# A two-layer diffusion backbone in full fp32: the q-half swap issued by another engine, one more gating half in the last head, and a lagging third projection at the norm boundaries

## Chip, cores, metric

One Trainium2 chip; the kernel runs on one core of it. The metric is the device time of one execution in microseconds (us), given as the median of several runs. TensorE does the matrix products, ScalarE the activations and most copies out of PSUM, VectorE the elementwise work, GpSimd some elementwise work and DMA issues, SyncE only DMA issues.

## The reference, cut to what matters

Two layers work on 512 latent tokens and 256 context tokens of width 1024. In each layer three branches (spatial gating, attention, short convolution) share one projection of the normalised stream; they are gated, merged and projected back, and a convolutional feed-forward block follows. In the second layer the context only gives keys and values.

```python
h_lat = modulate(rmsnorm(x, norm1_g[l]), sh1, sc1)
z_lat = h_lat @ w_in[l]            # 1024 -> 512 u, 512 v, q, k, v, conv, gates
q_lat = apply_rope(qk_heads(z_lat[..., B_Q:B_K], q_norm_g[l]), cos, sin)
...
def diff_attention(q, k, v, lam):  # 8 heads; q and k are 2 x 64 wide, v 128
    s = jnp.einsum('bqahd,bkahd->bahqk', q, k).astype(jnp.float32) * (B_QK_DIM ** -0.5)
    p = jax.nn.softmax(s, axis=-1)
    a = (p[:, 0] - lam * p[:, 1]).astype(v.dtype)
    return jnp.einsum('bhqk,bkhe->bqhe', a, v)
...
def spatial_gating(u, v, ln_g, w_s, b_s):
    u = jax.nn.gelu(u)
    v = layernorm(jax.nn.gelu(v), ln_g)
    ...
y_b = (rmsnorm(attn, sub_g) * (1.0 - lam_init)).reshape(bn, tn, B_WIDTH)
m = g_a * (y_a @ wa) + g_b * (y_b @ wb) + g_c * (y_c @ wc)
```

## The kernel before

**Layout and precision.** Activations lie feature by token: a tile has 128 features on its partitions and up to 768 tokens (512 latent, 256 context) along its row. Every fp32 product is made of three matmuls in a reduced type on a value's high part and its remainder: high times high (L183), high weight times low activation (L184), low weight times high activation (L186). So every operand is split first: ScalarE copies the high part (`whi`, `hh`, `kT`, `qT`, `vh`, `ah`), VectorE subtracts it from the original (`wlo`, `hl`, `vl`, `al`). A score block has the high and low part of a 64-wide half in one 128-row contraction; the second of its two products needs the same q with the halves of the partitions swapped, which is what the q-half swap makes by DMA (L743): rows 0 to 63 of `qT[:, 0]` to rows 64 to 127 of `qT[:, 1]` and the other way round, 64x2x256 each.

**Weights.** They come in halves of 128x1024 in a fixed order: SyncE issues the load (L62, `wraw`), ScalarE writes `whi` (L83), VectorE `wlo` (L69). There are two raw buffers, so a later load waits for the subtraction of an earlier one. `split_to(n)` writes ScalarE's part of the halves up to n at that place of the program, `take` does it for the half that is needed and the next; with `late` set, VectorE's part is written at the next `low()`.

**Order.** Each engine executes its instructions in the order in which the program writes them; that order is made by hand and by `weave`, which takes generators of pieces of work, each with a total cost, and always continues the one that is least advanced in share of its total. SyncE, too, takes its DMA issues in program order.

**Attention, per head.** While head h computes its scores (`attn`), the projections of head h+1 are woven in (`project`). Then comes the turn to the next head: `qk_tr` transposes the scaled and rotated q and k in three chunks of 256 tokens (two of q in layer 1), woven with one filler, a half of the convolution branch (`c_fill`). A chunk of q is copied out of PSUM by ScalarE (L741) and swapped in two DMAs (L743), a chunk of k is copied by ScalarE twice (L747). `v_tr` transposes v and splits it (L780, L781). Then `attn` takes blocks of 128 queries: scores (L857), VectorE's row minimum (L864), ScalarE's exponential (L869), the difference of the two softmaxes, its transposes (`to_at`, with the copy L897 `ah` and L898 `al`) and the product with v (`av`). The last head has no projection to be woven with: it gets the remaining fillers, which are two halves of the gating branch (`vs`, N_VS = 2).

**After the heads.** `branch_a` (spatial gating: the other `vs` halves with their gelu L1063, u, the layer norm's statistics L1086 and L1087, the token mixing) is woven with `subln`, the norm of the attention's output: the squares of all heads (L953) are split (L170, L171), summed over features on TensorE (L968), scaled by VectorE (L973) and transposed (L977).

**Norm boundaries.** `boundary` stands between two blocks, three times in the program. First come the last three projections of the old block on the first part of the tokens and then on the second, with their residuals `resid` (L1179 and the squares behind it, `sq_acc` L323), those of the second part being put off in `todo`. Then, in eight steps k, the normalised stream of the first part is written tile by tile (`norm_apply`: `hh` on ScalarE L376, `hl` on VectorE L379), and the first three projections of the next block use each tile as it comes: `step(k, part, i)` is the product of tile k for projection i. Projections 0 and 1 follow tile by tile; the third lags. `both` holds at the two boundaries inside a layer, where both token parts go through the norm here; between the layers the second part, the context, is left to the attention's start. The second part's statistics (`norm_stat`) start at one of these steps.

Of the kernel before, what the change touches and what calls it, by code (L numbers as in the profile page):

```python
# [11 lines left out]
F32 = mybir.dt.float32  # L12
# [8 lines left out]
NL, NC, T, D = 512, 256, 768, 1024  # L21
# [9 lines left out]
N_HALF = 2 * (NH * 3 + 12 + 4 + 4 + 24 + 8 + 8 + 8 + 44 + 24)  # L31
N_ADA = 4 * 24
N_LAST = 3
N_VS = 2


def weave(*gens, tick=lambda: None):
# [92 lines left out]
class Net:  # L130
# [376 lines left out]
    def boundary(self, pool, l, which, xt, pkeys, segs, evac, tail, xb=None, tmpb=None):  # L507
        parts = self.parts()
        (ao, am, _), (bo, bm, _) = parts
        sc = self.scales(l, which)  # L510
        self.scales_set(sc, l, which)
        both = xb is None
        tmp = lambda: pool.tile([128, T], F32, tag="nsq", bufs=2, name="nt")
        rb = pool.tile([128, T], F32, tag="rb", bufs=1, name="rb")
        rbb = rb[:, bo:bo + bm] if both else xb[8]
        xa = [x[:, ao:ao + am] for x in xt]
        todo = []
        tkeys, ks, xs, resid = tail
        self.ws.late = True
        ws = [self.ws.take(*key, ahead=0 if i else len(tkeys) - 1) for i, key in enumerate(tkeys)]  # L520
        m0 = 8 - len(tkeys)
        for i, w in enumerate(ws):
            ps = self.mm.tile([128, 512], F32, tag="mm", name="mm")
            self.gemm(w, ks, xs, [parts[0]], [ps])
            resid(m0 + i, parts[0], ps)
        for i, w in enumerate(ws):
            ps = self.mm.tile([128, 512], F32, tag="mm", name="mm")
            self.gemm(w, ks, xs, [parts[1]], [ps])
            todo.append(lambda i=i, ps=ps: resid(m0 + i, parts[1], ps))
            if i == 0:  # L530
                ra = self.norm_stat(ao, am)
                self.ws.split_to(len(self.ws.keys) + 1)
                self.defer = []
                todo.pop(0)()
                self.ws.low()
            if i == 1:
                self.norm_rows(rb[:, ao:ao + am], ra, am)
                self.ws.split_to(len(self.ws.keys) + 2)
        self.norm_h()
        step, finish = self.halves(pkeys, segs, evac)  # L540
        ga = self.norm_apply(tmp, sc, xa, rb[:, ao:ao + am], parts[0])
        next(ga)
        self.ws.low()
        self.ws.split_to(len(self.ws.keys) + 3)
        l1, l2 = 1, 2
        for k in range(8):
            if k == 1:
                self.ws.low()
            if both:
                step(k, parts[0], 0)  # L550
                step(k, parts[0], 1)
                if k:
                    step(k - 1, parts[0], 2)
            else:
                for i, lag in enumerate((0, l1, l2)):
                    if k >= lag:
                        step(k - lag, parts[0], i)
            if todo:
                todo.pop(0)()
            if k < 7:  # L560
                next(ga)
            for f in self.defer:
                f()
            self.defer = []
            if k == 3:
                r = self.norm_stat(bo, bm, True)
            if k == 6 and both:
                self.tick(99)
                self.norm_rows(rbb, r, bm)
        self.tick(99)  # L570
        self.defer = None
        if both:
            step(7, parts[0], 2)
        else:
            finish(parts[0], (8, 8 - l1, 8 - l2))
            self.norm_rows(rbb, r, bm)
        self.ws.low()
        self.ws.late = False
        gb = self.norm_apply(tmp if both else tmpb, sc, [x[:, bo:bo + bm] for x in xt] if both else xb, rbb, parts[1])
        if both:  # L580
            for k in range(8):
                next(gb)
                for i, lag in enumerate((0, 2, 4)):
                    if k >= lag:
                        step(k - lag, parts[1], i)
            finish(parts[1], (8, 6, 4))
            gb = None
        return gb
# [134 lines left out]
    def qk_tr(self, l, h, pool, st):  # L723
        nc = self.nc
        qT = pool.tile([128, 2, 2, T], F32R, tag="qT", bufs=1, name="qT")
        kT = [self.slots.tile([128, T], F32R, tag=f"B{1 + a}", name="kT") for a in range(2)]
        y = self.qk_rope(l, 2, pool, st)
        yield 1500
        for c in range(3):
            qs, ks = st.pop(("rope", c))  # L730
            t0 = c * 256
            for v, src in enumerate((qs, ks)):
                if src is None:
                    continue
                pt = self.mm.tile([128, 512], F32R, tag="mm", name="mmT")
                for a in range(2):
                    for b in range(2):
                        nc.tensor.transpose(pt[:, (2 * a + b) * 128:(2 * a + b + 1) * 128], src[:, 2 * b + a, :], self.identr)
                pf = pt.bitcast(F32)
                if v == 0:  # L740
                    nc.scalar.copy(qT[:, 0, :, t0:t0 + 256], pf.rearrange("p (a t) -> p a t", a=2))  # L741
                    for i, j in ((0, 64), (64, 0)):
                        nc.sync.dma_start(qT[i:i + 64, 1, :, t0:t0 + 256].bitcast(F32),  # L743
                                          qT[j:j + 64, 0, :, t0:t0 + 256].bitcast(F32))
                else:
                    for a in range(2):
                        nc.scalar.copy(kT[a][:, t0:t0 + 256], pf[:, 256 * a:256 * a + 256])  # L747
            if c == 0:
                st["rope", 2] = self.qk_hl(*y, pool)
            yield 1700  # L750
        st["q"], st["k"] = qT, kT
# [44 lines left out]
    def c_fill(self, l, pool, scr):  # L796
        nc = self.nc
# [39 lines left out]
            nc.sync.dma_start(scr[i][:, :n], c[:, :n])  # L837
        self.vg = []
        for i in range(N_VS):
            v = self.slots.tile([128, T], F32, tag=("B0", "B7")[i], name="vg")  # L840
            self.vg.append(v)
            yield half(0, i, lambda o, m, q: nc.scalar.copy(v[:, o:o + m], q[:, :m]), "vs")

# [407 lines left out]
    def run(self):  # L1251
        tc, nc, d = self.tc, self.nc, self.d
# [12 lines left out]
        with tc.tile_pool(name="const", bufs=1) as const, tc.tile_pool(name="w", bufs=1) as wp, \  # L1265
# [45 lines left out]
            for l in range(2):  # L1311
# [12 lines left out]
                with tc.tile_pool(name="attn", bufs=1) as ap, tc.tile_pool(name="pmm", bufs=4, space=PSUM) as self.mm, \  # L1324
# [3 lines left out]
                    tick = self.ws.low  # L1328
# [45 lines left out]
                    for h in range(8):  # L1374
                        a = self.attn(l, h, ap, st[h]), sum(self.attn_costs(l))
                        if h < 7:
                            weave(a, (project(h + 1), 23500), tick=tick)
                            turn(h + 1)
                        else:
                            weave(a, (fill(99), (1 + N_VS) * (6000 if l else 10000)), tick=tick)  # L1380
                self.ws.low()
                self.ws.late = False
                mmp = psum_all()
# [187 lines left out]
```

## Time and profile before

| | before |
|---|---|
| time, median of 3 runs | 2674.5 us (2672.96, 2674.5, 2675.52) |
| the profiled execution's own time | 2675.01 us |
| its span | 2673.2 us |
| granted TensorE clock, mean over the span | 0.993 of full speed |
| TensorE matmul busy | 2617.0 us, 98% |
| TensorE weight load busy (beside the matmuls) | 2267.7 us, 85% |
| VectorE busy | 1631.2 us, 61% |
| ScalarE busy | 1035.2 us, 39% |
| GpSimd busy | 220.9 us, 8% |

The span runs from the first to the last instruction on record; the execution's time has 1.8 us around it. Busy shares are means over the whole span; what a stage waits for is read from the waits and the timelines of that stage. In a timeline's row stand the start in us from the span's start, the length, the engine, the line with the operation, what it writes and reads with shapes, and in brackets the idle time in front of it with what ended it. DMA-issuing instructions aren't counted as busy.

### The profile page before, as it was taken

What the parts mean: (1) busy time and instruction counts of PE and PEld (TensorE: products, weight loads), DVE (VectorE), ACT (ScalarE), POOL (GpSimd) and SP (SyncE); (2) the same over time, 40 slices, a digit from 0 to 9 for tenths busy, and PEclk for the clock granted to TensorE, in tenths of its full rate; (3) what the DMA queues carried; (4) which work ended last, traced back from release to release, by engine and by line L of the source; (5) the groups of instructions that cost most, each with busy time, mean ns of one, the idle gap of its engine ahead of it and who ended that gap; (6) DMA issues with size and microseconds to landing.
All of it is one profiled execution on the core that took longest, in us unless ns stands there. A gap on an engine that the chain in (4) does not pass through costs nothing.

```text
span 2673.2 us, 37362 instructions
## 1 busy us (share of the span) xinstructions
PE 2617.0 (98%) x15128; PEld 2267.7 (85%) x15128; DVE 1631.2 (61%) x2887; ACT 1035.2 (39%) x1840; POOL 220.9 (8%) x202
## 2 busy tenths in 40 slices
PE   7999999999999999999999999999999999999999
PEld 3899999888888888888888878898978888888887
DVE  5677777656546447544544567777767564654544
ACT  3455555542121224312312335555563232343422
POOL 0000000001111111100100100000001121010101
PEclk8999999999999999999999999999999999999999
DMA  5212221224333332222222232212125554233233
GB/s 224 82 44 58 64 66 44 66 66 149 113 116 111 103 127 66 76 87 72 79 81 77 91 100 67 68 55 63 53 75 173 175 163 175 71 99 100 94 103 110
DMA packets 79660, 254.36 MB, mean 95 GB/s; under 512 B 9200, under 2 KB 19712, under 8 KB 79104
## 3 DMA queue, kind: packets, MB, share of 16 engines
q1 hardware_dynamic: 64512, 196.64, 23.1%
q0 software_dynamic: 14544, 55.07, 6.4%
q8 instruction: 119, 1.95, 0.3%
q14 instruction: 53, 0.43, 0.1%
q10 hardware_dynamic: 432, 0.27, 0.0%
HBM read 234.63 MB, written 6.82 MB: 90 GB/s over the span
## 4 chain that ended last, share of the span: by engine, by line
PE 82%; DVE 10%; ACT 4%; DMA 2%; issue 1%; SPq 0%; POOL 0%; ACTq 0%; POOLq 0%; DVEq 0%
PE mm L183 22%; PE mm L186 22%; PE mm L184 22%; PE S L857 3%; PE mm L647 2%; PE mm L649 2%; PE mm L648 2%; DVE wlo L69 2%; PE mmT L893 1%; ACT whi L83 1%; DMA qT<-qT 1%; ACT pa L869 1%; DVE zs L697 1%; DVE al L898 1%; PE mmT L906 1%
## 5 line engine op out<-in xcount | busy, mean ns | idle before, releaser
L183 PE MATMUL mm<-hh,whi 128*128 128x512 f32 (+1 forms) x2392 | 855.3, 358 | 12.1 <-ACT hh L376 10.2
L184 PE MATMUL mm<-hl,whi 128*128 128x512 f32 (+1 forms) x2392 | 820.0, 353 | 4.4 <-DVE hl L379 4.1
L186 PE MATMUL mm<-hh,wlo 128*128 128x512 f32 (+1 forms) x2392 | 752.6, 353 | 1.6 <-DVE wlo L69 1.6
L183 PEld LDWEIGHTS mm<-hh,whi 128*128 128x128 f32 x2392 | 452.6, 189 | 104.5 <-ACT hh L376 14.4
L69 DVE TENSOR_TENSOR wlo<-wraw,whi 128x1024 fp32r<-128x1024 f32 x320 | 399.4, 1249 | 195.8 <-ACT whi L83 194.2
L184 PEld LDWEIGHTS mm<-hl,whi 128*128 128x128 f32 x2392 | 453.3, 190 | 68.4 <-DVE hl L379 9.3
L186 PEld LDWEIGHTS mm<-hh,wlo 128*128 128x128 f32 x2392 | 415.1, 190 | 42.1 <-DVE wlo L69 3.7
L83 ACT CAST whi<-wraw 128x1024 fp32r<-128x1024 f32 x320 | 335.0, 1048 | 285.0 <-PE mm L184 243.4
L1018 DVE SCALAR_TENSOR_TENSOR cv<-mm,pc,cv 128x511 f32<-128x511 f32 (+1 forms) x132 | 86.8, 658 | 181.7 <-ACT cv L1017 180.8
L869 ACT ACTIVATE pa<-S,mn 128x768 f32<-128x768 f32 (+1 forms) x160 | 129.3, 813 | 153.1 <-DVE mn L864 125.7
L183 PE MATMUL mm<-ah,whi 128*128 128x512 f32 (+1 forms) x528 | 187.9, 356 | 0.0
L647 PE MATMUL mm<-whi,hh 128*128 128x256 f32 x640 | 183.0, 286 | 1.3 <-DVE cp L794 0.8
L648 PE MATMUL mm<-wlo,hh 128*128 128x256 f32 x640 | 180.7, 282 | 0.0
L649 PE MATMUL mm<-whi,hl 128*128 128x256 f32 x640 | 180.6, 282 | 0.0
L184 PE MATMUL mm<-al,whi 128*128 128x512 f32 (+1 forms) x528 | 179.9, 354 | 0.0
L186 PE MATMUL mm<-ah,wlo 128*128 128x512 f32 (+1 forms) x528 | 161.7, 355 | 0.0
L1017 ACT ACTIVATE cv<-mm,pc 128x512 f32<-128x512 f32 (+1 forms) x132 | 88.7, 705 | 177.2 <-PE mm L186 177.2
L1179 DVE SCALAR_TENSOR_TENSOR x<-mm,mod,x 128x512 f32<-128x512 f32 (+1 forms) x91 | 58.2, 659 | 139.0 <-PE mm L186 139.0
L1222 POOL TENSOR_TENSOR cv<-cv 128x768 f32<-128x768 f32 (+1 forms) x44 | 91.9, 2088 | 607.3 <-DVE cv L1020 420.7
L857 PE MATMUL S<-kT,qT 128*128 128x512 f32 x576 | 118.2, 341 | 10.1 <-DMA qT<-qT 8.7
L647 PEld LDWEIGHTS mm<-whi,hh 128*128 128x128 f32 x640 | 121.9, 190 | 4.3 <-ACT cp L792 1.0
L864 DVE TENSOR_REDUCE mn<-S 128x1 f32<-128x768 f32 x128 | 116.1, 949 | 10.3 <-PE S L857 10.3
(237 smaller groups left out, 4035.9 us busy)
## 6 DMA issues: line engine op xcount, KB each, us to landing
wraw<-w SPq DMA_DIRECT2D x320, 512.0 KB, 3.6
araw<-ada POOLq DMA_DIRECT2D x80, 512.0 KB, 4.0
qT<-qT SPq DMA_DIRECT2D x80, 128.0 KB, 3.8
araw<-ada SPq DMA_DIRECT2D x16, 512.0 KB, 8.3
x<-xT SPq DMA_DIRECT2D x8, 384.0 KB, 7.7
srow<-sscr POOLq DMA_DIRECT2D x3, 1024.0 KB, 5.5
x<-xT POOLq DMA_DIRECT2D x8, 384.0 KB, 6.2
xscr<-x SPq DMA_DIRECT2D x8, 256.0 KB, 3.9
```

Of the source, the lines that this page charges most:

```text
L69: self.lo_eng.tensor_tensor(lo, raw, hi.bitcast(F32), ALU.subtract)
L83: self.nc.scalar.copy(hi, raw)
L183: nc.tensor.matmul(ps[:, :m], lhsT=hh, rhs=xh[:, o:o + m], start=st, stop=False)
L184: nc.tensor.matmul(ps[:, :m], lhsT=hh, rhs=xl[:, o:o + m], start=False, stop=False)
L186: nc.tensor.matmul(ps[:, :m], lhsT=hl, rhs=xh[:, o:o + m], start=False, stop=sp)
L647: nc.tensor.matmul(ps[:, :256], lhsT=hh[:, sl], rhs=hi[:, c:c + 256], start=(k == 0), stop=False)
L648: nc.tensor.matmul(ps[:, :256], lhsT=hh[:, sl], rhs=lo[:, c:c + 256], start=False, stop=False)
L649: nc.tensor.matmul(ps[:, :256], lhsT=hl[:, sl], rhs=hi[:, c:c + 256], start=False, stop=(k == 7))
L857: nc.tensor.matmul(s[:, c0 + o:c0 + o + m], lhsT=st["q"][:, v, a, t0:t0 + 128], rhs=st["k"][a][:, k0 + o:k0 + o + m], start=(v == 0), stop ...
L864: nc.vector.tensor_reduce(mn[:, a:a + 1], ss[a], AX.X, ALU.min)
L869: nc.scalar.activation(pa[:, :nk], ss[a], AF.Exp, bias=mn[:, a:a + 1], scale=-1.0, accum_out=sm[a])
L1222: nc.gpsimd.tensor_tensor(cs[1][:, :n], cs[1][:, :n], cs[0][:, :n], ALU.mult)
```

## The change

Four edits:

- The swap's two DMAs are issued by ScalarE, behind its copy L741, instead of SyncE.
- N_VS is 3: the third `vs` half is a filler of the last head and not a part of `branch_a`; the last head's fillers get another total in `weave`.
- At the boundaries the third projection lags by three tiles in all cases (before by two, with `both` by one); the cast of its weights is no longer written ahead of the steps.
- There too, the put-off residuals are written at steps 2 and 3 (before at the first steps), and the second part's statistics at step 4 (before 3).

```diff
-N_VS = 2
+N_VS = 3
...
         next(ga)
         self.ws.low()
-        self.ws.split_to(len(self.ws.keys) + 3)
-        l1, l2 = 1, 2
+        l1, l2 = 1, 3
         for k in range(8):
             if k == 1:
                 self.ws.low()
             if both:
                 step(k, parts[0], 0)
                 step(k, parts[0], 1)
-                if k:
-                    step(k - 1, parts[0], 2)
+                if k >= l2:
+                    step(k - l2, parts[0], 2)
...
-            if todo:
+            if todo and k in (2, 3):
                 todo.pop(0)()
...
-            if k == 3:
+            if k == 4:
                 r = self.norm_stat(bo, bm, True)
...
         if both:
-            step(7, parts[0], 2)
+            for k in range(8 - l2, 8):
+                step(k, parts[0], 2)
...
                     for i, j in ((0, 64), (64, 0)):
-                        nc.sync.dma_start(qT[i:i + 64, 1, :, t0:t0 + 256].bitcast(F32),
-                                          qT[j:j + 64, 0, :, t0:t0 + 256].bitcast(F32))
+                        nc.scalar.dma_start(qT[i:i + 64, 1, :, t0:t0 + 256].bitcast(F32),
+                                            qT[j:j + 64, 0, :, t0:t0 + 256].bitcast(F32))
...
-            v = self.slots.tile([128, T], F32, tag=("B0", "B7")[i], name="vg")
+            v = self.slots.tile([128, T], F32, tag=("B0", "B7", "B2")[i], name="vg")
...
-                            weave(a, (fill(99), (1 + N_VS) * (6000 if l else 10000)), tick=tick)
+                            weave(a, (fill(99), N_VS * 10.4 * (512 if l else 768)), tick=tick)
```

ScalarE, in the turn to a head of layer 0 (`qT`, `kT` are the transposed q and k of a chunk, `mmT` the PSUM tile of their transposes, `cc<-cp,pc` the convolution of the filler):

```order
 L1015 ACTIVATE cc<-cp,pc_85 128x512
 L741 CAST qT<-mmT 128x2x256
-L747 CAST kT<-mmT 128x256 x2
-L741 CAST qT<-mmT 128x2x256
+L743 DMA qT<-qT 64x2x256 x2
+L747 CAST kT<-mmT 128x256 x2
+L741 CAST qT<-mmT 128x2x256
+L743 DMA qT<-qT 64x2x256 x2
 L747 CAST kT<-mmT 128x256 x2
 L1015 ACTIVATE cc<-cp,pc_85 128x256
```

Two issues now stand between each copy of q and the copies of k behind it.

TensorE, in the same turn, at the third chunk (`identr` is the identity of the transposes; in brackets the semaphores that the instruction waits for):

```order
 L738 MATMUL mmT<-identr,qs 128x128 [waits DVE_49,Activation_49]
 L738 MATMUL mmT<-identr,qs 128x128 x3
-L738 MATMUL mmT<-identr,ks 128x128 [waits DVE_49,PE_49,Activation_49]
+L738 MATMUL mmT<-identr,ks 128x128 [waits DVE_49]
 L738 MATMUL mmT<-identr,ks 128x128 x3
 L183 MATMUL mm<-hh,whi 128x256
```

The transposes of k wait for VectorE alone, since their PSUM tile is another buffer than before.

VectorE, after the attention of layer 1, where `branch_a` and `subln` are woven. Before:

```order
L171 TENSOR_TENSOR sql<-ssq,sqh 128x512 x5
L69 TENSOR_TENSOR wlo<-wraw,whi 128x1024
L171 TENSOR_TENSOR sql<-ssq,sqh 128x512 x3
L69 TENSOR_TENSOR wlo<-wraw,whi 128x1024
L973 TENSOR_SCALAR srs<-ssum 8x512
L1086 BN_STATS st_19413<-vt 128x6
L1087 BN_AGGR mv<-st_19413 128x2
```

In the changed kernel, around the same L973:

```order
L161 TENSOR_TENSOR rst<-rst,rsn 128x4
L163 SCALAR_TENSOR_TENSOR rsy<-rst,rsy 128x4
L1092 TENSOR_SCALAR vt<-vt,mv,rsy 128x512 x4
L69 TENSOR_TENSOR wlo<-wraw,whi 128x1024
L973 TENSOR_SCALAR srs<-ssum 8x512
L981 MEMSET sry 128x512
L983 SCALAR_TENSOR_TENSOR srs<-sm_95 128x32
```

The scaling of the sums (L973) stood ahead of the layer norm's statistics (L1086 to L1092) and stands behind them now, and behind one more L69. On TensorE the last sum L968 stands right ahead of the transposes L977 that need L973, in both layers, and the first L968 comes right behind the last `vs` half.

ScalarE, at the norm boundary within layer 0 (`hh<-nt,mod` is the normalised tile, `rb<-st` the row of the norms, `nsb<-x` the square of a residual's result):

```order
 L351 COPY rb<-st 128x512
 L83 CAST whi<-wraw 128x1024
-L376 ACTIVATE hh<-nt,mod_87 128x512
-L83 CAST whi<-wraw 128x1024
+L376 ACTIVATE hh<-nt,mod_87 128x512 x3
 L323 ACTIVATE nsb<-x 128x256
 L376 ACTIVATE hh<-nt,mod_87 128x512
+L83 CAST whi<-wraw 128x1024
 L323 ACTIVATE nsb<-x 128x256
-L376 ACTIVATE hh<-nt,mod_87 128x512 x6
+L376 ACTIVATE hh<-nt,mod_87 128x512 x4
```

The third projection's weights (the second L83) stood behind one `hh` and stand behind four; the squares moved down by two.

## Rows read from the trace of the kernel before

**Rows 1.** The page's first part: the span, and each engine's busy time, share and instructions.

```profile
span 2673.2 us, 37362 instructions
...
PE 2617.0 (98%) x15128; PEld 2267.7 (85%) x15128; DVE 1631.2 (61%) x2887; ACT 1035.2 (39%) x1840; POOL 220.9 (8%) x202
```

**Rows 2.** The waits of TensorE's matmuls over the whole span, by what ended them: sum in us, count, longest.

```profile
PE mm L183 <- ACT hh L376: 10.2, 8, 2.2
...
PE S L857 <- DMA qT<-qT: 8.7, 7, 1.5
...
PE mmT L905 <- ACT ah L897: 4.3, 3, 3.2
...
PE S L857 <- ACT pa L869: 1.4, 6, 0.2
```

**Rows 3.** The instructions of line 743, the swap's issues on SyncE (SPq), and of line 1287, the only two loads that ScalarE's queue (ACTq) issues before: shortest, median and longest in ns, and where in the span.

```profile
L743 SPq DMA_DIRECT2D qT<-qT x80: 590/605/1403, 117.1 to 1957.0; - x80
...
DMA to landing us min/median/max: 2.3/3.8/5.5
...
L1287 ACTq DMA_DIRECT2D pc<-pcol x2: 335/335/335, 7.1 to 8.3; - x2
```

**Rows 4.** ScalarE's timeline in a turn of layer 0, from 168 to 182 us.

```profile
170.56 0.41 ACT L716 CAST qs<-ry 128x256 fp32r<-128x256 f32 x1 [1.37 <-DVE ry L708]
...
171.80 0.56 ACT L741 CAST qT<-mmT 128x512 fp32r<-128x512 f32 x1
...
172.99 0.59 ACT L741 CAST qT<-mmT 128x512 fp32r<-128x512 f32 x1
173.54 0.65 ACT L747 CAST kT<-mmT 128x256 fp32r<-128x256 f32 x2
...
174.48 1.05 ACT L83 CAST whi<-wraw 128x1024 fp32r<-128x1024 f32 x1
...
176.20 0.86 ACT L780 CAST vh<-mmT 128x512 fp32r<-128x512 f32 x2 [0.67 <-PE mmT L778]
...
179.15 0.91 ACT L869 ACTIVATE pa<-S,mn 128x768 f32<-128x768 f32 x1 [2.09 <-DVE mn L864]
```

**Rows 5.** VectorE's timeline in the same turn.

```profile
173.57 0.69 DVE L818 TENSOR_TENSOR cc<-cc,mm 128x512 f32<-128x512 f32 x1
...
176.11 1.22 DVE L69 TENSOR_TENSOR wlo<-wraw,whi 128x1024 fp32r<-128x1024 f32 x1
...
177.24 1.01 DVE L781 TENSOR_TENSOR vl<-mmT,vh 128x512 fp32r<-128x512 f32 x2
178.17 1.81 DVE L864 TENSOR_REDUCE mn<-S 128x1 f32<-128x768 f32 x2
```

**Rows 6.** TensorE's timeline in the same turn.

```profile
172.97 0.54 PE L738 MATMUL mmT<-identr,ks 128*128 128x128 f32 x4
...
180.50 1.57 PE L857 MATMUL S<-kT,qT 128*128 128x512 f32 x8
```

**Rows 7.** A turn of layer 1: ScalarE's, VectorE's and TensorE's timelines between 1680 and 1693 us.

```profile
1682.11 0.41 ACT L719 CAST ks<-ry 128x256 fp32r<-128x256 f32 x1 [0.83 <-DVE ry L708]
...
1684.05 0.65 ACT L747 CAST kT<-mmT 128x256 fp32r<-128x256 f32 x2
...
1684.57 1.09 ACT L83 CAST whi<-wraw 128x1024 fp32r<-128x1024 f32 x1
...
1689.50 0.90 ACT L869 ACTIVATE pa<-S,mn 128x768 f32<-128x768 f32 x1 [3.08 <-DVE mn L864]
...
1688.52 1.81 DVE L864 TENSOR_REDUCE mn<-S 128x1 f32<-128x768 f32 x2
...
1687.49 1.29 PE L857 MATMUL S<-kT,qT 128*128 128x512 f32 x6 [1.46 <-DMA qT<-qT]
```

**Rows 8.** The end of layer 0's last head: TensorE's timeline, and the stretch from 522 to 527 us by windows. The columns of the second row are the stretch, its length, the busy us of PE, PEld, DVE, ACT and POOL (with instructions), the granted TensorE clock, the DMA engines' share and GB/s.

```profile
522.67 0.39 PE L905 MATMUL mmT<-ah,vh 128*128 128x256 f32 x1 [3.22 <-ACT ah L897]
...
522.00:527.00 5.00, 3.99 (x22) 3.67 (x22) 1.80 (x5) 1.37 (x6) 0.00 (x0) 0.76 0.08 30
```

**Rows 9.** After the attention of layer 1: the timelines of ScalarE, VectorE and TensorE between 1992 and 2019 us.

```profile
1999.87 0.59 ACT L1063 ACTIVATE vg<-mm 128x512 f32<-128x512 f32 x1
...
2001.01 0.62 ACT L170 CAST sqh<-ssq 128x512 fp32r<-128x512 f32 x1
...
2004.04 0.69 DVE L171 TENSOR_TENSOR sql<-ssq,sqh 128x512 fp32r<-128x512 f32 x1 [0.49 <-ACT sqh L170]
...
2007.20 0.68 DVE L973 TENSOR_SCALAR srs<-ssum 8x512 f32<-8x512 f32 x1 [0.99 <-PE ssum L968]
...
2015.80 1.22 DVE L69 TENSOR_TENSOR wlo<-wraw,whi 128x1024 fp32r<-128x1024 f32 x1
...
2014.33 0.41 PE L977 MATMUL ssum<-ident,srs 8*128 8x8 f32 x4
```

**Rows 10.** The three norm boundaries: TensorE's wait at the second normalised tile of each, ScalarE's cast of the third projection's weights at the first of them, and the windows of the second boundary from 1573 to 1581 us (columns as in rows 8).

```profile
1007.14 0.51 PE L183 MATMUL mm<-hh,whi 128*128 128x512 f32 x1 [1.37 <-ACT hh L376]
...
1574.59 0.50 PE L183 MATMUL mm<-hh,whi 128*128 128x512 f32 x1 [2.25 <-ACT hh L376]
...
2299.90 0.38 PE L183 MATMUL mm<-hh,whi 128*128 128x256 f32 x1 [1.83 <-ACT hh L376]
...
1005.12 1.04 ACT L83 CAST whi<-wraw 128x1024 fp32r<-128x1024 f32 x1 [1.81 <-DMA wraw<-w]
...
1573.00:1581.00 8.00, 4.78 (x10) 2.78 (x11) 6.64 (x12) 3.59 (x7) 0.00 (x0) 0.68 0.42 131
```

## The prediction

> **What bounds the kernel now.** TensorE. The page gives it 2617.0 us of a span of 2673.2 [rows 1], so no edit that leaves its matmuls as they are can win more than the 56 us in which it idles. The wait table of TensorE says what those are [rows 2]: 10.2 us behind hh, the normalised tile that ScalarE writes at the norm boundaries; 8.7 us behind the q-half swap qT<-qT, in seven waits; 4.3 us behind ah in the last head; and behind ScalarE's exponentials (L869) 1.4 us in six waits of 0.2, small, but a sign that the score blocks run with almost no slack against ScalarE. I then read, stage by stage, the timelines of ScalarE, VectorE and TensorE around those waits, and the order of instructions in both kernels. No matmul is added or removed, so the whole sum is about waits.
>
> **Swap from ScalarE's queue: what an issue costs.** The swap's 80 issues hold SyncE for 590 to 1403 ns, median 605 [rows 3]. No qT issue of ScalarE is in the trace; its two pcol issues take 335 ns [rows 3], but they are of another shape (128 plain rows against 64x2x256). The price on ScalarE is thus bounded by 0.34 and 0.61 us, and I take 0.60, the row of the same transfer. ScalarE is in order, the first issue of a pair waits for the copy in front of it (L741), and L747 and all behind it wait for the pair: about 2 x 0.60 and 0.13 us, an estimate of mine for the first issue's wait until the copy has ended, so 1.33 us for a pair, three pairs a head in layer 0 and two in layer 1. SyncE gets the 0.6 us back, and nobody waits for SyncE's weight loads in these stages, so that is worth nothing.
>
> **Layer 0, eight heads.** Here the swap ends no wait of TensorE at all, so there is nothing to win. The turn at 168 to 182 us: pair one disappears in the idle 1.37 us ahead of L716 [rows 4]. Pair two pushes the third L741 from 172.99 to about 174.3. Pair three pushes the last L747 (173.54 plus 0.65) to an end near 176.9, L83 from 174.48 to 177.1, and L780 from 176.20 to 178.2, the idle 0.67 in front of it being used up. VectorE's L69 needs that L83: it goes from 176.11 to about 178.2, and behind it L781, the minimum L864 (178.17) and then the exponential L869 (179.15) go by the same 2.1 us [rows 4, 5]. TensorE's next score block stands at 180.50 [rows 6], 0.44 us behind the end of that exponential (179.15 plus 0.91); the block after it has no such slack, it is one of the six waits of 0.2. So the head ends 2.1 us later. Inside this lies a second loss that needs no issue price: the order shows that the third ks transpose takes another PSUM buffer and now waits for VectorE alone. What VectorE frees there is the fill's first half, read by L818 until 174.26 [rows 5], while TensorE wants it at 172.97 [rows 6]: 1.3 us. It is not added, since the block behind waits for the longer of the two. 8 x 2.1 = **+17 us**; bounds +4 (0.34 us an issue) and +22.
>
> **Layer 1, eight heads.** Here the swap does end a wait: the score block stops for 1.46 us until 1687.49 [rows 7]. With the issue right behind the copy the halves land earlier. But two pairs, less the idle 0.83 us in front of L719, push the last L747 from 1684.05 by 1.9 us, to an end near 1686.6, and the second and fourth score matmuls read that kT. So TensorE resumes near 1686.9, not at 1685.9: 0.6 of the 1.46 us is won. L83 (1684.57) goes by 1.9 us as well, VectorE's L69, L781 and L864 follow it, L864 from 1688.52 to 1689.7 and L869 from 1689.50 to 1690.7 [rows 7]. The later blocks of the head hang on that chain (scores, L864, L869, scores), so they end up to 1.2 us later, and the early gain is lost in it. I take +0.9 a head, near the chain's shift: 8 x 0.9 = **+7 us**; bounds -6 (most of the 8.7 us won) and +12. What is late next, in both layers, is ScalarE.
>
> **Third gating half in the last head.** The 4 us behind ah in layer 0, the longest of them 3.22 us, go, since filler matmuls now stand between the head's last blocks; the granted clock of 522 to 527 us is 0.76 of full speed [rows 8], the lower level for a part of it, which gives 1.2 us more (0.24 of the 5.00). But the half is missing after the attention. There it covered ScalarE's squares: in the new order the first L968 comes right behind the last gating half, and ScalarE must first do L1063, L953 and L170, in layer 1 1.8 us (1999.87 to 2001.63, [rows 9]), with the split's 0.5 us behind it. And VectorE's L973, done at 2007.20 before, now stands behind the statistics and the L69 that ends at 2017.02, while TensorE wants its result at 2014.33 [rows 9]: 2.7 us, plus 0.68 for L973, less 0.7 that the chain starts earlier. Layer 1: +5. Layer 0, 768 columns for 512: 2.6 + 0.5, and 1.3 for L973 behind the last L968, less 4 and 1.2: -1. Together **+4 us**; bounds -4 and +9.
>
> **Norm boundaries.** At each of the three, TensorE waits at the second hh: 1.37, 2.25 and 1.83 us [rows 10], because L83 of the third projection stands in front of it and waits for its weights to land (1.81 us of idle at 1005.12). The new order puts three hh ahead of this L83. These 5.4 us go, and 0.6 behind them on hl. The second wait of each boundary is the residual, the sum and an L69 on VectorE; they are moved two steps down, not removed, and with the third projection lagging TensorE has two matmul groups a step to cover them, not three. I give 1 us back for that: **-5 us**; bounds -10 (the granted clock is 0.68 of full speed from 1573 to 1581 us [rows 10], and could recover) and 0.
>
> **The sum.** 17 + 7 + 4 - 5 = +23 us. The profiled execution itself took 2675.0 us (span 2673.2 and 1.8 around it), 0.5 above the median of the runs; 2675.0 + 23 = 2698.0, as a median about 2697.5.
>
> **Rivals.**
> *An issue on ScalarE is cheap* (0.34 us or less). For it: the pcol rows. Against: they are as long as SyncE's plain ones, so the engine is not the difference, the shape is. Then a pair costs 0.8, layer 0 loses at most the 1.3 us of the PSUM buffer in some heads, some 6 us, layer 1 wins 2, the rest stays at 4 - 5: 2678, from 2672 to 2690. It decides where a pair falls below about 0.8 us.
> *Faster: the waits simply go.* The mechanism is ScalarE's slack: if its 2.09 and 3.08 us of idle ahead of L869 [rows 4, 7] swallow the pairs and nothing behind them moves, then 8.7 us of swap waits, the 4 us in the last head and 5 to 6 at the boundaries go: 2675 - 18 = 2657. Against: the idle time is there because L869 waits for VectorE, and VectorE waits for ScalarE's L83; the shift goes through it.
> *Issues collide.* The 1403 ns row [rows 3] is an issue that found something in its way. If the first issue of each head meets one of SyncE's weight loads, which now run on the other queue at the same time, it costs 0.8 us more: 16 x 0.8 = 13, 2711. The Trainium skill (Perfetto Trace Analysis, DMA Instruction - HWDGE) says that descriptor generation is locked for exclusive use, and that an issuing engine's window includes the wait for this lock, with its sequencer held until it ends; by that rule the collision is what happens. No row of before has two queues issuing in these stages. New stalls of 2 us and more can also cost granted clock, as the old one at 522 us did, in the same direction.
> That the change doesn't do what it says can be excluded: the order shows each edit.
>
> **How the numbers follow.** Forecast 0.66 (2690 to 2708); cheap issue 0.17, of which 0.09 slower, 0.07 the same, 0.01 faster; faster 0.08; collisions 0.09. A measurement of this kernel can tell about 0.2%, 5.3 us, from no change. So slower 0.84, same 0.07, faster 0.09. The range, 2677 to 2712, takes in the bounds of the issue price and leaves out the faster rival, the lower part of the cheap one and part of the collisions.
>
> **What would show it.** Right: qT issues of about 600 ns on ScalarE; the swap gone from TensorE's waits, and L857 behind kT and L869, L738 behind VectorE in its place; head periods of layer 0 some 2 us and of layer 1 some 1 us longer; new waits of L968 and L977; hh waits down by about 5 us. Wrong: ScalarE's issues at a third of a microsecond, or head periods unchanged, which would take the attention's 24 us out of the sum.

## The result and the profile after

The changed kernel takes 2702.22 us (median of 4 runs, 2700.74 to 2702.99) against 2675.01 us of the kernel before (4 runs): a ratio of 1.0102, 95% interval 1.0089 to 1.0116, so 27 us slower, between 24 and 31. The prediction was +23 us, 2697.5.

The page's first part, as in [rows 1]:

```profile
span 2699.0 us, 37312 instructions
...
PE 2623.9 (97%) x15128; PEld 2263.6 (84%) x15128; DVE 1629.4 (60%) x2887; ACT 1035.9 (38%) x1842; POOL 221.3 (8%) x202
```

The same matmuls, in a span longer by 25.8 us: for 6.9 of them TensorE is busy longer, in the rest it idles. TensorE's wait table, to be read against [rows 2]:

```profile
PE S L857 <- ACT pa L869: 15.7, 28, 1.7
PE mm L184 <- DVE hl L379: 6.8, 14, 1.5
...
PE mm L183 <- ACT hh L376: 4.5, 6, 1.1
PE mmT L738 <- DVE ks L720: 4.3, 7, 1.4
PE ssum L968 <- ACT sqh L170: 4.3, 2, 2.4
PE mmT L738 <- DVE cc L818: 4.2, 4, 1.4
PE ssum L977 <- DVE srs L973: 4.1, 2, 2.8
...
PE mmT L738 <- ACT kT L747: 2.9, 2, 1.5
...
PE mmT L905 <- ACT ah L897: 0.7, 1, 0.7
...
PE S L857 <- DMA qT<-qT: 0.3, 1, 0.3
```

The swap's 8.7 us and the 4.3 us behind ah have all but gone, and hh has halved. In their place stand the score blocks behind the exponential (1.4 us before, 15.7 now), the transposes L738 and the two waits L968 and L977 of the attention's norm.

A table by stage says more than the sums. For the same TensorE matmul in each trace, this is how much later than in the kernel before each stage ended, as a difference to the stage ahead of it, in us (worked out from the start times in the traces; what differs ahead of the first stage, 1 us or less, is left out; the forecast's -5 for three boundaries is split by thirds). The last columns are runs told below.

| stage, by the kernel before's time | predicted | after | swap_only | third_half_only | boundary_only | swap_later |
|---|---|---|---|---|---|---|
| layer 0, seven turns (123 to 491) | +17 | +16.7 | +16.6 | -0.1 | -0.1 | +7.5 |
| its last head and gating (to 605) | -1 | +0.9 | +2.7 | -1.4 | +0.9 | +1.2 |
| two norm boundaries (to 1602) | -3.3 | -5.7 | -0.5 | -1.6 | -5.7 | -1.1 |
| up to layer 1's first scores (to 1641) | 0 | -2.2 | +1.0 | -0.1 | -1.0 | -1.4 |
| layer 1, seven turns (to 1959) | +7 | +10.0 | +9.6 | +0.3 | +0.1 | +2.3 |
| its last head and gating (to 2100) | +5 | +7.5 | +2.2 | +5.9 | +0.4 | +0.4 |
| third boundary (to the end) | -1.7 | -2.1 | +0.1 | +0.3 | -2.2 | +0.3 |

Each column is one execution, and the granted clock differs between executions in places that no edit touches: the +2.7 of swap_only in layer 0's last head has no added wait (TensorE idles 4.5 us there in both kernels), and the row up to 1641 lies between -2.2 and +1.0 with the same work in all of them.

**A turn of layer 0.** The turn of [rows 4 to 6]; it begins 2.2 us later here. First ScalarE's timeline:

```profile
170.85 1.26 ACTq L743 DMA_DIRECT2D qT<-qT  x2
...
174.54 1.26 ACTq L743 DMA_DIRECT2D qT<-qT  x2
175.84 0.65 ACT L747 CAST kT<-mmT 128x256 fp32r<-128x256 f32 x2 [1.33 <-PE mmT L738]
...
177.01 1.26 ACTq L743 DMA_DIRECT2D qT<-qT  x2
178.59 0.65 ACT L747 CAST kT<-mmT 128x256 fp32r<-128x256 f32 x2 [1.61 <-issue]
179.12 0.52 ACT L1015 ACTIVATE cc<-cp,pc 128x256 f32<-128x256 f32 x1
179.53 1.05 ACT L83 CAST whi<-wraw 128x1024 fp32r<-128x1024 f32 x1
```

VectorE's and TensorE's timelines of the same turn:

```profile
179.68 0.48 DVE L1018 SCALAR_TENSOR_TENSOR cc<-cp,pc,cc 128x255 f32<-128x255 f32 x1 [3.27 <-ACT cc L1015]
...
180.78 0.42 DVE L818 TENSOR_TENSOR cc<-cc,mm 128x256 f32<-128x256 f32 x1
181.12 1.22 DVE L69 TENSOR_TENSOR wlo<-wraw,whi 128x1024 fp32r<-128x1024 f32 x1
...
183.19 1.81 DVE L864 TENSOR_REDUCE mn<-S 128x1 f32<-128x768 f32 x2
...
176.46 0.53 PE L738 MATMUL mmT<-identr,ks 128*128 128x128 f32 x4 [1.36 <-DVE cc L818]
...
185.21 0.97 PE L857 MATMUL S<-kT,qT 128*128 128x512 f32 x4 [1.09 <-ACT pa L869]
```

ScalarE waits for the issue, VectorE waits 3.27 us for ScalarE's L1015, and everything up to the minimum L864 comes 2.8 us later than in [rows 5], counted from the turn's beginning. TensorE stops at the third ks transposes for 1.36 us and at the second score block for 1.09.

**Behind the attention of layer 1**, to be read against [rows 9]: TensorE's and VectorE's timelines, and the windows of the stretch (columns as in rows 8).

```profile
2020.91 0.50 PE L968 MATMUL ssum<-sqh,zsel 128*128 128x512 f32 x1 [1.85 <-ACT sqh L170]
...
2042.07 0.67 DVE L973 TENSOR_SCALAR srs<-ssum 8x512 f32<-8x512 f32 x1
...
2042.79 0.59 PE L977 MATMUL ssum<-ident,srs 8*128 8x8 f32 x4 [2.79 <-DVE srs L973]
```

```profile
2020.00:2060.00 40.00, 36.04 (x169) 29.72 (x170) 25.49 (x62) 18.83 (x31) 4.16 (x5) 0.91 0.23 72
```

Both waits are there, and with them a granted clock of 0.91 over 40 us, which costs some 3 us more: 0.09 of the 36 us in which TensorE is busy.

### The profile page after: what moved, and what is told of

The parts are those of the page before. It is cut to its first block, busy times and chain, and to the rows that moved or that the text cites. A ratio compares the mean times of both kernels' runs of the same rounds, so it can differ in the third digit from the quotient of the medians.

```text
span 2699.0 us, 37312 instructions
## 1 busy us (share of the span) xinstructions
PE 2623.9 (97%) x15128; PEld 2263.6 (84%) x15128; DVE 1629.4 (60%) x2887; ACT 1035.9 (38%) x1842; POOL 221.3 (8%) x202
## 3 DMA queue, kind: packets, MB, share of 16 engines
q8 instruction: 119, 1.95, 0.3%
## 4 chain that ended last, share of the span: by engine, by line
PE 73%; DVE 13%; ACT 9%; ACTq 2%; issue 2%; DMA 1%; SPq 0%; DVEq 0%
PE mm L183 20%; PE mm L186 20%; PE mm L184 20%; DVE wlo L69 2%; PE S L857 2%; ACT whi L83 2%; ACT pa L869 2%; ACTq L743 2%; PE mm L647 2%; PE mm L649 2%; PE mm L648 2%; DVE mn L864 1%; PE mmT L893 1%; ACT kT L747 1%; DVE ry L706 1%
## 5 line engine op out<-in xcount | busy, mean ns | idle before, releaser
L69 DVE TENSOR_TENSOR wlo<-wraw,whi 128x1024 fp32r<-128x1024 f32 x320 | 397.7, 1243 | 215.5 <-ACT whi L83 212.1
L83 ACT CAST whi<-wraw 128x1024 fp32r<-128x1024 f32 x320 | 334.9, 1048 | 281.3 <-PE mm L184 243.6
L1018 DVE SCALAR_TENSOR_TENSOR cv<-mm,pc,cv 128x511 f32<-128x511 f32 (+1 forms) x132 | 86.8, 657 | 181.3 <-ACT cv L1017 180.4
L869 ACT ACTIVATE pa<-S,mn 128x768 f32<-128x768 f32 (+1 forms) x160 | 129.3, 813 | 152.5 <-DVE mn L864 124.7
L857 PE MATMUL S<-kT,qT 128*128 128x512 f32 x576 | 124.2, 349 | 16.4 <-ACT pa L869 15.7
L648 PEld LDWEIGHTS mm<-wlo,hh 128*128 128x128 f32 x640 | 122.1, 191 | 1.0 <-DVE wlo L69 0.9
```

Source lines behind the costliest of these rows:

```text
L69: self.lo_eng.tensor_tensor(lo, raw, hi.bitcast(F32), ALU.subtract)
L83: self.nc.scalar.copy(hi, raw)
L648: nc.tensor.matmul(ps[:, :256], lhsT=hh[:, sl], rhs=lo[:, c:c + 256], start=False, stop=False)
L857: nc.tensor.matmul(s[:, c0 + o:c0 + o + m], lhsT=st["q"][:, v, a, t0:t0 + 128], rhs=st["k"][a][:, k0 + o:k0 + o + m], start=(v == 0), stop ...
L869: nc.scalar.activation(pa[:, :nk], ss[a], AF.Exp, bias=mn[:, a:a + 1], scale=-1.0, accum_out=sm[a])
```

## The experiments

Each of these was timed against the kernel before on the same chip; its medians there lay between 2673.7 and 2676.8 us. Gains and losses in us are worked out from the ratios, as shares of 2675 us.

**swap_only, burn, third_half_only, boundary_only: the parts alone.** The first, third and fourth take one part of the diff each. burn leaves the swap on SyncE and has ScalarE copy a constant instead:

```diff
+                    burn = pool.tile([128, 512], F32, tag="burn", bufs=1, name="burn")
                     for i, j in ((0, 64), (64, 0)):
+                        nc.scalar.copy(burn, self.ones[:, 0:1].to_broadcast([128, 512]))
                         nc.sync.dma_start(qT[i:i + 64, 1, :, t0:t0 + 256].bitcast(F32),
```

> Only the swap goes to ScalarE's queue; fillers and boundaries as before. My theory: its price is ScalarE's own time behind the copies (two issues of 0.6 us a pair), so +24 us by the prediction's terms (17 in layer 0, 7 in layer 1), about 2699. The changed kernel's trace has +17 and +10 over the heads, so 2699 to 2702. Rival: the whole change costs +27 because its parts act on each other (the third gating half or the boundaries make the heads longer); then the swap alone stays under +15.

> The swap stays on SyncE; behind each copy of q ScalarE does two copies of a constant, 128x512 each (about 0.56 us), that nobody reads. My theory (ScalarE's time is the price): layer 0 loses as much as with the swap on ScalarE, about 2 us a head and 15 in all; layer 1 loses the same time and does not get the earlier landing, so at least +7 there: 2695 to 2705. Rival (the price lies in the queue: issues of two queues in each other's way, or another landing): within 3 us of before, 2672 to 2678.

> Only the third gating half moves to the last head. The prediction's term: +4 us (-1 in layer 0, +5 in layer 1), 2679. The changed kernel's trace has +1 and +9 there, of which some 5 us is a lower granted clock behind the new waits: if those belong to the moved half alone, +10, 2685. If the extra 6 us come only together with the swap, +4.

> Only the boundaries change. The prediction's term: -5 us, 2670. The changed kernel's trace has about -9 to -11 there, since the granted clock no longer falls at the boundaries: 2665. If the waits on hh are only exchanged for others: 2674 to 2676.

| | median us | ratio to before | 95% interval |
|---|---|---|---|
| swap_only | 2704.93 | 1.0105 | 1.0088 to 1.0122 |
| burn | 2693.41 | 1.0067 | 1.0052 to 1.0082 |
| third_half_only | 2679.80 | 1.0017 | 1.0008 to 1.0026 |
| boundary_only | 2667.27 | 0.9973 | 0.9961 to 0.9984 |

The parts add up: +28, +4.5 and -7 make +25.5, inside the interval of the whole. The swap is the loss (+24 to +27 had been expected of it). In burn the copies' group of instructions on ScalarE reads

```profile
L744 ACT COPY burn<-ones 128x512 f32<-128x512 f32 x80 | 50.0, 625 | 1.3
```

so a pair costs about what two issues do, and no DMA changed its queue; still 18 of the 28 us are lost, 14.0 of 16.6 in layer 0. That speaks against the rival that put the price into the queue. In layer 1 it lost only 4.1 us, not the 7 that I had expected, and the whole lies just under the 2695 to 2705 named.

**swap_gpsimd: the swap on an idle engine's queue.**

```diff
-                        nc.sync.dma_start(qT[i:i + 64, 1, :, t0:t0 + 256].bitcast(F32),
+                        nc.gpsimd.dma_start(qT[i:i + 64, 1, :, t0:t0 + 256].bitcast(F32),
```

> The swap is issued by GpSimd, which has nothing else to do in the heads; the rest as before. My theory (ScalarE's time is the price, the early landing is a gain): no loss in layer 0 and part of the 8.7 us of swap waits won in layer 1, 2665 to 2674. Rival (the second queue is the price: its transfers and SyncE's weight loads get in each other's way): the heads are longer as with ScalarE's queue, by 10 us or more. A third way: GpSimd takes longer than SyncE to get a swap landed (3.8 us there); then TensorE's wait behind qT grows above 8.7 us, and layer 0, where nothing waited, stays unchanged up to some slack.

2676.80 us, ratio 1.0004 (0.9993 to 1.0015): no difference. From the rows of line 743 and TensorE's wait table:

```profile
L743 POOL DMA_DIRECT2D qT<-qT x80: 587/589/608, 115.5 to 1960.4; - x80
...
DMA to landing us min/median/max: 2.3/4.4/6.4
```

```profile
PE S L857 <- DMA qT<-qT: 9.9, 7, 2.0
```

The seven turns of layer 0 are unchanged to 0.1 us: another queue as such costs nothing there. But the swap lands no earlier than from SyncE [rows 3], and the 8.7 us stay. The gain that the early landing was to bring in layer 1 did not exist for this queue; the expectation's third way came true, with 2.5 us more in layer 1's turns of this one execution.

**third_half_squares_first: the two new waits of the attention's norm.** As third_half_only, with another weave:

```diff
-weave((self.branch_a(l, pp), 62000 - 7800 * N_VS), (self.subln(l, pp), 20000))
+weave((self.subln(l, pp), 17000), (self.branch_a(l, pp), 62000 - 7800 * N_VS))
```

> Only the third gating half is moved, as in the run with that edit alone, but the norm of the attention's output is woven first and with a total of 17000 for 20000: ScalarE's squares then stand ahead of the gelus, and VectorE's L973 ahead of the layer norm's statistics. My theory: the loss of the moved half is the 4.3 us behind the squares' split (L968) and the 4.1 us behind L973; without them the half's gain in the last head (4 us behind ah, and clock) is left: -3 to -8 us, 2666 to 2671. Rival: gelus and squares only change places, and the waits go to the transposes behind the gelus: 2675 to 2682, as before this edit.

2669.29 us, ratio 0.9977 (0.9967 to 0.9987): -6 us where the same edit without the weave has +4.5. The waits at L968 and L977 are gone from the table, and the windows have full clock in layer 0's last head, where [rows 8] had 0.76, and behind layer 1's, where third_half_only had 0.91 from 2000 to 2040 us (in the first of the two places it, too, had full clock):

```profile
1985.00:2025.00 40.00, 39.18 (x195) 31.89 (x194) 25.98 (x64) 24.60 (x40) 5.22 (x7) 1.00 0.32 99
522.00:527.00 5.00, 5.00 (x31) 4.24 (x30) 1.42 (x3) 1.12 (x3) 0.00 (x0) 1.00 0.36 107
```

One detail of the expectation was wrong: in layer 1, L973 still stands behind the statistics and an L69. It no longer hurts because its reader L977 now comes behind other work of TensorE. In layer 1 the moved half then neither wins nor loses (+0.3); the gain is layer 0's 5.9.

**swap_later, swap_old_buffers, new_buffers_only: which part of the swap's move is the price.** swap_later is swap_only with the two issues of a chunk written behind its copies of k:

```diff
                 else:
                     for a in range(2):
                         nc.scalar.copy(kT[a][:, t0:t0 + 256], pf[:, 256 * a:256 * a + 256])
+            if qs is not None:
+                for i, j in ((0, 64), (64, 0)):
+                    nc.scalar.dma_start(qT[i:i + 64, 1, :, t0:t0 + 256].bitcast(F32),
```

> As the run with the swap alone on ScalarE, but the two issues of a chunk stand behind its two copies of k and not ahead of them; the PSUM buffers of the transposes are then those of the kernel before. My theory (what counts is the ScalarE time ahead of the filler's L1015 and the weight cast L83, on which VectorE's L69 and the row minima wait): layer 0 still loses 13 to 16 us and layer 1 about 9, 2696 to 2700. Rival (the late copies of k and the other PSUM buffer, at which the transposes stop for 1.4 us, are the price): no waits at L738 any more, and 7 us or more of the 28 are gone: 2690 or less.

2684.44 us, ratio 1.0028 (1.0018 to 1.0038): +7.5, not +23 to +27. The expectation failed and the rival's number came out. But two things had changed at once, since the PSUM buffers were now those of the kernel before. So the buffers were fixed by hand, one tag for each of the four banks, in the order recorded from the one kernel or the other:

```diff
+    def tile(self, shape, dt, tag, name):
+        return self.pool.tile(shape, dt, tag="mm" + next(self.seq), name=name)
```

> The swap on ScalarE right behind the copy of q, as in the run with the swap alone, but the PSUM buffers of the attention are fixed to those of the kernel before, tile by tile. It tells apart why the issues behind the copies of k cost 9 us and those ahead of them 28. If the other PSUM buffer is the price: 2685 to 2690, near the run with the later issues. If it is ScalarE's time (ahead of the copies of k the two issues stand alone, behind them they run beside the copies): 2698 to 2705, as the swap alone; the transposes then wait for the copies of k instead of VectorE.

> The counterpart: the swap stays on SyncE, and the PSUM buffers of the attention are fixed to those of the run with the swap alone. If the buffers are the price: +10 us or more, with 1.3 us waits of the third ks transposes behind VectorE's L818. If ScalarE's time is: at most the 1.3 us in the turns where VectorE frees the buffer late, less what the blocks behind had as slack: 0 to +5 us, 2674 to 2680.

| | median us | ratio to before | 95% interval |
|---|---|---|---|
| swap_later | 2684.44 | 1.0028 | 1.0018 to 1.0038 |
| swap_old_buffers | 2702.97 | 1.0099 | 1.0083 to 1.0116 |
| new_buffers_only | 2684.17 | 1.0027 | 1.0017 to 1.0036 |

With the old buffers the swap costs 26.5 us, as much as with the new ones; the buffers alone cost 7, more than the 0 to 5 expected and less than their rival's 10. They aren't added: in swap_old_buffers the transposes stop just as long, behind another engine (line 753 there is 738 here):

```profile
176.30 0.54 PE L753 MATMUL mmT<-identr,ks 128*128 128x128 f32 x4 [1.44 <-ACT kT L762]
```

So it is ScalarE's time after all: swap_old_buffers and swap_later have the same buffers and the same issues, and differ by 19 us through the issues' place alone. swap_later shows how little time an issue need take. ScalarE's timeline there (its lines 744, 747 and 1016 are 747, 743 and 1015 here):

```profile
175.05 0.38 ACT L744 CAST kT<-mmT 128x256 fp32r<-128x256 f32 x1
175.18 0.60 ACTq L747 DMA_DIRECT2D qT<-qT  x1
175.31 0.39 ACT L744 CAST kT<-mmT 128x256 fp32r<-128x256 f32 x1
175.81 0.64 ACTq L747 DMA_DIRECT2D qT<-qT  x1
176.50 0.51 ACT L1016 ACTIVATE cc<-cp,pc 128x256 f32<-128x256 f32 x1 [0.79 <-issue]
```

The issue at 175.18 runs while the copies of k execute: its own input, the copy of q, was done. The pair exposes 0.79 us here and 1.61 in the changed kernel, where the issue has to wait for the copy right ahead of it and the copies of k come behind both issues.

**no_swap_squares_first and all_gpsimd: the best of the parts.** The changed kernel with the swap on SyncE's queue and the weave of third_half_squares_first; then the same with the swap on GpSimd's queue.

```diff
-                        nc.scalar.dma_start(qT[i:i + 64, 1, :, t0:t0 + 256].bitcast(F32),
+                        nc.sync.dma_start(qT[i:i + 64, 1, :, t0:t0 + 256].bitcast(F32),
...
-weave((self.branch_a(l, pp), 62000 - 7800 * N_VS), (self.subln(l, pp), 20000))
+weave((self.subln(l, pp), 17000), (self.branch_a(l, pp), 62000 - 7800 * N_VS))
```

> The changed kernel with the swap back on SyncE's queue and the norm of the attention's output woven first with a total of 17000. By the parts: -7 (boundaries alone, measured) and -3 to -8: 2659 to 2665, faster than both kernels. If the parts share their gain (the granted clock, above all), 2664 to 2668.

> The same with the swap on GpSimd's queue. If GpSimd's swap wins the layer-1 waits: another -3 to -8 us, 2653 to 2660. If it lands later than SyncE's: slower than the kernel with SyncE's swap by what TensorE waits more behind qT, 2665 or more.

2659.24 us, ratio 0.9937 (0.9925 to 0.9950), and 2662.71 us, ratio 0.9947 (0.9935 to 0.9960). The first is 17 us faster than the kernel before (its parts alone give -13, which their intervals don't tell from 17), and 43 faster than the change. GpSimd's queue adds nothing; its 2662.71 lies between the two outcomes that I had named.

## Why the prediction was right

**The price of an issue.** Taken as 0.60 us from the row of the same transfer and not 0.34 from the plain loads: measured on ScalarE

```profile
L743 ACTq DMA_DIRECT2D qT<-qT x80: 597/615/1648, 115.7 to 1977.1; - x80
...
DMA to landing us min/median/max: 2.3/2.5/5.3
```

The engine isn't the difference, as argued: 605 ns on SyncE, 615 on ScalarE, 589 on GpSimd. What a pair costs ScalarE came out as forecast too: 1.33 us of idle time ahead of L747 behind the second pair of the turn shown above (the view puts it down to the transposes L738, which had long ended), and 1.61 behind the third.

**Layer 0, +17 forecast, +16.7 measured, but by two errors that cancel.** The chain was the right one, and up to L83 and L780 each step was met to 0.2 us. Then the step "VectorE's L69 needs that L83" missed a wait: VectorE's convolution of the filler (L1018, L1020, L818) stands ahead of L69 and needs ScalarE's second L1015, which comes behind the last pair. So L69 and the minima come 2.8 us later, not 2.1. From one turn's beginning to the next's, four turns lose 2.6 to 2.8 us, and three, whose filler has no convolution there, 1.6 to 1.7. The eighth costs 1.3, since the last head's fillers cover the rest. That the sum was met to 0.3 us is luck. The PSUM buffer's loss was rightly not added: new_buffers_only has it as 7 us by itself, and swap_old_buffers doesn't miss it.

**Layer 1, +7 forecast, +10.0 measured.** The early gain was indeed lost in the chain: the swap's waits fell from 8.7 to 0.3 us, and the block behind waits for L869 instead. The chain's shift was sized too low. ScalarE and TensorE in the turn that answers to [rows 7]:

```profile
1691.37 1.93 ACTq L743 DMA_DIRECT2D qT<-qT  x2
1693.34 0.65 ACT L747 CAST kT<-mmT 128x256 fp32r<-128x256 f32 x2 [2.00 <-issue]
...
1694.81 0.54 PE L738 MATMUL mmT<-identr,ks 128*128 128x128 f32 x4 [1.05 <-DVE ks L720]
...
1697.79 1.08 ACT L83 CAST whi<-wraw 128x1024 fp32r<-128x1024 f32 x1
...
1703.75 1.50 PE L857 MATMUL S<-kT,qT 128*128 128x512 f32 x6 [1.24 <-ACT pa L869]
```

The turn begins 10.6 us later than in [rows 7]. So L83, which stands there at 1684.57, comes 2.6 us later by this turn's doing, not 1.9. Counted in the same way, L83 moves by 1.8 to 2.0 us in the turns behind it, as forecast, but for one with 2.8. These two turns have a long issue each (here the first pair takes 1.93 us), and in them the transposes wait 1.05 and 1.41 us for a split of k (L720) behind ScalarE's L719, which the pair had delayed; elsewhere 0.4. The sum had no such wait. The other step that was too small is VectorE's: the minimum L864 was to go by 1.2 us, less than L83, and here goes by 2.6, as much as L83, because the filler's convolution stands ahead of L69 in this turn, too. So it does in two of the six turns behind it (1.95 us each); in the others L864 goes by 1.0 to 1.3, and by 2.3 in the one with the long issue. The last head comes on top, with 2.2 us more in swap_only.

The second issue of that pair takes 1292 ns. That is the collision rival's size, but in 2 of 80 issues, some 2 us in all and not 13. The rival's condition was met all the same: in 15 of the 16 turns ScalarE's second issue begins 0.12 to 0.15 us after SyncE has begun to issue a weight load, while that issue (0.33 us) still runs. 13 of these 15 take 620 to 632 ns, against about 598 of the issue ahead of them. The two long ones of the kernel before (1029 and 1403 ns) came 0.18 us behind the end of a weight load's issue, on SyncE's own queue; a second queue is thus not needed for a long one. The lock of the descriptor generator that the Trainium skill describes (Perfetto Trace Analysis, DMA Instruction - HWDGE) may be in it; no row here shows the lock.

**Third gating half, +4 forecast; +4.5 measured alone.** Both waits were there with their sizes: L977 2.79 us in layer 1, where 2.7 and 0.68 less 0.7 were summed, and L968 1.85 and 0.23 where 2.3 was. Alone, layer 0 won 1.4 (forecast 1) and layer 1 lost 5.9 (forecast 5). Two things that the term left out work against each other there, which is luck: the granted clock behind the new waits, some 3 us, and 1.6 us that come back at 2042 us, where the kernel before stops twice and this one doesn't:

```profile
2042.43 0.50 PE L183 MATMUL mm<-yh,whi 128*128 128x512 f32 x1 [0.55 <-ACT whi L83]
...
2043.69 0.50 PE L186 MATMUL mm<-yh,wlo 128*128 128x512 f32 x1 [0.53 <-DVE wlo L69]
```

**Norm boundaries, -5 forecast; -7 measured alone, -7.8 by the stages in the changed kernel.** The direction was right and the mechanism only in part. Of hh 5.7 us went, and 2.7 came back behind hl (6.8 us above); that makes -3, not the -5 of the waits that I had summed. The kernel before has

```profile
PE mm L184 <- DVE hl L379: 4.1, 10, 1.5
```

The rest is clock, which stood in the bounds and not in the sum. The windows around the three boundaries, the kernel before, then boundary_only:

```profile
1000.00:1030.00 30.00, 26.69 (x128) 20.99 (x128) 22.30 (x48) 11.90 (x20) 0.00 (x0) 0.94 0.18 53
...
1560.00:1590.00 30.00, 25.23 (x128) 20.01 (x127) 21.89 (x51) 11.39 (x17) 0.54 (x1) 0.89 0.28 93
...
2285.00:2315.00 30.00, 25.99 (x182) 24.40 (x180) 18.53 (x57) 9.85 (x20) 0.00 (x0) 0.89 0.19 59
```

```profile
1000.00:1030.00 30.00, 27.92 (x152) 22.20 (x151) 25.25 (x56) 13.45 (x24) 0.00 (x0) 1.00 0.17 53
...
1560.00:1590.00 30.00, 26.14 (x137) 20.53 (x136) 22.01 (x55) 13.26 (x19) 0.54 (x1) 1.00 0.21 71
...
2285.00:2315.00 30.00, 26.33 (x182) 23.84 (x182) 23.19 (x67) 12.26 (x24) 0.00 (x0) 0.94 0.16 53
```

The clock rises from 0.94, 0.89 and 0.89 to 1.00, 1.00 and 0.94; in the changed kernel it is the same to 0.01. What that is worth shows between the same matmuls ahead of and behind each boundary (960 to 1040, 1555 to 1602 and 2270 to 2335 us of the kernel before). These three stretches take 7.8 us less in the changed kernel: TensorE idles 3.2 us less and needs 4.6 less for the same matmuls, which is the clock. The edit's doing is clear of the clock's own variation: they sum to 184.0 to 184.6 us in the four traces with the edit and to 189.8 to 192.6 in the nine without it.

**The sum, +23 forecast, +27 measured.** By the stages the terms come to +16.7, +10.0, +8.4 and -7.8, and -2.2 up to 1641 us, where no term stood. Of the +8.4 only 4.5 is the gating half's by itself; the rest stands in the same stages of swap_only. So layer 1 and the last heads were forecast 7 us too low, the boundaries and the stretch behind them 5 too high: that the whole came this near is in part luck.

**The rivals.** Cheap issues: the engine's rows say no, yet swap_later comes to +7.5 with the same issues of 0.6 us, where that rival had +6 and -2 for the swap. The pair there exposes 0.79 us, which is the point from which that rival was to decide; the place of the issue can bring it there, which the prediction didn't see. The faster rival fell as argued, since ScalarE's idle time ahead of L869 was a wait for a chain through ScalarE itself.

**burn in layer 1.** It loses 4 us where the swap costs 10. Its pair takes 0.27 us less of ScalarE, so with two pairs a turn L83 moves by 1.2 to 1.4 us, 0.55 less than above, which is some 4 us in seven turns; and it has no long issue on ScalarE, another 2. That is the difference.

**Open.** Why just two of the 15 issues are long no run shows. They come in the same two turns of layer 1 as the two long ones of the kernel before, which SyncE issued.

## What to carry to other kernels

A DMA issue on a compute engine takes a place in that engine's line. In this kernel a pair was cheap (0.79 us, +7.5 in all) where its input was ready and the engine had something else to execute meanwhile, and dear (1.3 to 1.6 us, +26.5) right behind the instruction that makes its input. Follow a delayed instruction on every engine to the next joint chain, and look at what stands ahead of its reader in that engine's own order: here the filler's convolution turned 2.1 us into 2.8. Work moved into a gap leaves a gap where it stood; in this kernel one reordering of the work that lost its cover turned +4.5 us into -6.

## What the runs showed of the hardware

- An engine executes instructions while its queue issues a DMA that stands behind them: in swap_later an issue of 0.60 us begins 0.13 us after a copy of 0.38 us has begun, and the next copy begins 0.13 us after that.
- The same 64x2x256 swap holds SyncE for 605, ScalarE for 615 and GpSimd for 589 ns, and lands after 2.5 us (median) from ScalarE, 3.8 from SyncE and 4.4 from GpSimd.
- At the boundaries the waits that went were worth 3.2 us and the granted clock that came back with them 4.6.
- Two queues that issued at once mostly cost each other little: of the 15 swap issues of ScalarE that began while SyncE was issuing a weight load, 13 took 620 to 632 ns, and two 1292 and 1648.
